# The first two k tiles' modulation taken singly, with a new written order for the opening of a two-layer block kernel

## The chip, the cores and the metric

The kernel runs on one core of one Trainium2 chip. The metric is device time of one execution in microseconds (us), the median of several runs; a profiled execution of the same kernel gives the trace. The core has TensorE (PE; its weight loads are shown apart as PEld), VectorE (DVE), ScalarE (ACT), GpSimd (POOL) and SyncE (SP), which here issues most of the transfers.

## The reference, cut to what matters

The reference is two layers of a diffusion block over 256 latent tokens and 256 context tokens of width 1024: in each layer a gated feed-forward stage, a mixer (a short convolution in layer 0, grouped attention in layer 1) and a second feed-forward stage. Before each stage the tokens are normed and modulated by vectors that come from a conditioning vector. The change touches the opening: the first modulation, norm and feed-forward product of layer 0.

```
def _rms(t, g):
    t32 = t.astype(jnp.float32)
    y = t32 * lax.rsqrt(jnp.mean(t32 * t32, axis=-1, keepdims=True) + NORM_EPS)
    return y.astype(t.dtype) * g
def _modulate(t, g, shift, scale):
    return _rms(t, g) * (1 + scale) + shift
def _swiglu(h, w13, w2):
    gte, up = jnp.split(h @ w13, 2, axis=-1)
    return (jax.nn.silu(gte) * up) @ w2
...
        mod = (jax.nn.silu(c) @ mod_w[i] + mod_b[i]).reshape(bsz, 3, 3, 1, D_MODEL)
        modc = (jax.nn.silu(c_ctx) @ mod_w[i] + mod_b[i]).reshape(3, 3, D_MODEL)
        lat = lat + 0.5 * mod[:, 0, 2] * _swiglu(_modulate(lat, norm_g[i, 0], mod[:, 0, 0], mod[:, 0, 1]), ffn_w13[i, 0], ffn_w2[i, 0])
```

The same weights serve latent tokens (with `c`) and context tokens (with `c_ctx`), so every modulation product has two rows.

## The kernel before

Tokens lie transposed: `x` is [128, 8, 512], that is eight k tiles of 128 features with 256 latent and 256 context tokens side by side. Every fp32 product is made of three products of rounded halves: an operand is split into a high part (`wh`, `hh`; ACT) and the rest (`wl`, `hl`; DVE), and high x high, high x low and low x high are added up in PSUM.

The first feed-forward stage begins with three w13 blocks, i = 0, 1, 2, each with two PSUM tiles, `pg` and `pu`. Their products go over eight k tiles, taken as q = 0..3 (pairs) and j = 0, 1, with k = 2q + j.

Elsewhere a scheduler sets the order of instructions; in this opening a hand-written order does, the string `FIRST_STEPS` (L39), for TensorE, VectorE, ScalarE and the SP queue. Each engine runs its instructions in that order, and a waiting one holds up all behind it. A step is a letter with digits:

- `L` chq: `mod_load` (L913), two transfers of 512 KB with the columns of modulation chunk ch (0 is shift, 1 is scale) for the two k tiles of pair q, from `in_mod0`.
- `P` chq: `mod_pe` (L918), the product of these 256 columns with the conditioning vector. The eight k slices of the contraction go to four 32-column strips of the array (`tile_position`), in two rounds; fp32 takes two passes each, so one P is 16 passes of 256 columns. ACT then copies the result to `row`.
- `T` chq: `mod_turn` (L934), two small products per pair with `rowsum` that add the four strips and turn the row into columns; DVE adds the bias and writes `A00` (1 + scale) or `B00` (shift, named `mod` in the trace).
- `R` i half: `first_raw` (L1020), a 512 KB transfer of half a w13 block. `W` i p: `first_w` (L1031), the split of 512 of its columns, one ACT and one DVE instruction.
- `X`: `first_inv` (L950), the inverse rms spread over the partitions by PE, and ACT's copies of it, `ris`, for the two token halves.
- `U` q: `scale_q` (L958), x times norm gain times `ris` on DVE, four instructions for a pair, into `hr`.
- `N` qj: `norm_one` (L968), the modulated tile of one k: ACT writes `hh`, DVE (or ACT, for j = 1 and q > 0) the full value, DVE the rest `hl`.
- `h`, `w`, `l` with iqj: `first_part` (L994), two products each for one k tile: high x high, low weights, low tokens. `M` iq: all twelve of block i and pair q.
- `F` and the `WARM` matmuls before the list: `fill` (L894), products of a tile of ones into an unused PSUM tile, two passes each. `S` loads the conditioning vectors for later.

Before the list come the fill and `rms_sum` (L270), which sums squares with PE and takes root and reciprocal. PSUM has a pool of six tiles (`psum`) and one of two (`psmall`). The two sums lie in the small pool until ACT has copied `ris`; P10's result goes to the large pool, P00's to the small one.

## Time and profile before

| | |
|---|---|
| median of 3 runs | 1567.11 us (1566.95 to 1568.15) |
| profiled execution | 1566.27 us |
| its span in the profile | 1564.5 us |
| TensorE clock granted | 1.00 |
| read from memory | 259.45 MB, 167 GB/s over the span |

In the trace each group of instructions has its line, engine, output and inputs; times are from the start of the span. A matmul's time includes its way through the array, so neighbours overlap, and their spacing is taken from their starts or from the chain of waits, where each piece begins where the one before it ends. A few per cent of the matmul records can be missing.

### The profile page before, as it was taken

Reading aid. Unit: us, or ns where it says so; the run is one execution under the profiler, and the core shown is the slowest. Engines: PE = TensorE matmul, PEld = TensorE weight load, DVE = VectorE, ACT = ScalarE, POOL = GpSimd, SP = SyncE. Lnnn points to the kernel's source line nnn. Section 1 sums busy time; section 2 is a strip of 40 time slices with the busy share of each in tenths; the row PEclk is TensorE's granted clock in tenths of the full one; section 3 lists DMA queues with packets and bytes.
Section 4 is the critical chain, followed back from the end, with each engine's and each line's share of the span. In section 5 each row is a group of like instructions: output and inputs, shape, how many; then the busy total and the mean of one; then the engine's idle time right before and its main releaser. Section 6 shows DMA issues by size and latency. Waiting matters only on the chain.

```text
span 1564.5 us, 26382 instructions
## 1 busy us (share of the span) xinstructions
PE 1552.8 (99%) x10296; PEld 1422.4 (91%) x10296; DVE 1284.7 (82%) x2029; ACT 775.2 (50%) x1297; POOL 224.7 (14%) x188
## 2 busy tenths in 40 slices
PE   9999999999999999999999999999999999999999
PEld 7898998999888899989999899989999899898888
DVE  5789789889987588978978888978978788888676
ACT  5642453545323465436435475436445456674553
POOL 0012304100000111132131111131131002300000
PEclk9999999999999999999999999999999999999999
DMA  9567567564665525665665635665765743277562
GB/s 370 195 187 203 133 174 195 136 186 141 190 191 177 124 67 149 189 161 125 196 160 139 188 84 135 194 164 120 257 164 155 236 151 118 85 238 218 171 197 74
DMA packets 88254, 263.53 MB, mean 168 GB/s; under 512 B 10817, under 2 KB 12609, under 8 KB 88129
## 3 DMA queue, kind: packets, MB, share of 16 engines
q1 hardware_dynamic: 69408, 230.72, 46.1%
q0 software_dynamic: 16128, 29.37, 11.4%
q10 hardware_dynamic: 2592, 1.76, 0.4%
q8 instruction: 80, 1.31, 0.3%
q14 instruction: 46, 0.37, 0.1%
HBM read 259.45 MB, written 1.05 MB: 167 GB/s over the span
## 4 chain that ended last, share of the span: by engine, by line
PE 83%; DVE 9%; DMA 3%; ACT 2%; issue 2%; POOL 0%; POOLq 0%; DVEq 0%; ACTq 0%; SPq 0%
PE py L138 7%; PE py L137 7%; PE py L139 7%; PE p L137 6%; PE p L138 5%; PE p L139 5%; PE q L137 4%; PE q L139 4%; PE q L138 4%; DVE junk L178 2%; PE py L145 2%; PE pu L145 2%; PE pg L145 2%; DMA wr<-in_modT 2%; DVE wl L109 2%
## 5 line engine op out<-in xcount | busy, mean ns | idle before, releaser
L108 ACT ACTIVATE wh<-wr 128x1024 fp32r<-128x1024 f32 (+2 forms) x446 | 394.6, 913 | 329.6 <-PE py L138 123.3
L109 DVE TENSOR_TENSOR wl<-wr,wh 128x1024 fp32r<-128x1024 f32 (+2 forms) x446 | 459.0, 1053 | 91.6 <-ACT wh L108 73.0
L178 DVE CUSTOM_DVE_ANT_0 junk<-wr,scbc,modb 128x1024 bf16<-128x1024 f32 x213 | 275.0, 1291 | 49.3 <-DMA wr<-in_modT 46.8
L138 PE MATMUL py<-gl,wh 128*128 128x512 f32 (+1 forms) x570 | 213.4, 374 | 0.1
L137 PE MATMUL py<-gh,wh 128*128 128x512 f32 (+1 forms) x570 | 213.5, 375 | 0.0
L139 PE MATMUL py<-gh,wl 128*128 128x512 f32 (+1 forms) x570 | 213.0, 374 | 0.0
L704 POOL TENSOR_SCALAR wr<-wr 128x512 f32<-128x512 f32 x56 | 100.1, 1788 | 708.3 <-DMA wr<-in_w 474.4
L567 DVE SCALAR_TENSOR_TENSOR x<-py,mod,x 128x256 f32<-128x256 f32 x213 | 94.2, 478 | 51.8 <-PE py L139 40.8
L137 PE MATMUL p<-th,wh 128*128 128x256 f32 x448 | 126.8, 283 | 0.0
L138 PE MATMUL p<-tl,wh 128*128 128x256 f32 x448 | 126.8, 283 | 0.0
L139 PE MATMUL p<-th,wl 128*128 128x256 f32 x448 | 126.8, 283 | 0.0
L139 PEld LDWEIGHTS py<-gh,wl 128*128 128x128 f32 x570 | 107.3, 188 | 19.2
L138 PEld LDWEIGHTS py<-gl,wh 128*128 128x128 f32 x570 | 107.4, 188 | 18.5 <-DVE gl L109 0.5
L137 PEld LDWEIGHTS py<-gh,wh 128*128 128x128 f32 x570 | 107.4, 188 | 18.4
L115 POOL DMA_DIRECT2D w4l<-in_w x56 | 52.2, 932 | 283.2 <-ACT w4l L114 205.7
L137 PE MATMUL q<-bh,wh 128*128 128x256 f32 x320 | 90.9, 284 | 1.6 <-ACT wh L108 0.8
L139 PE MATMUL q<-bh,wl 128*128 128x256 f32 x320 | 90.9, 284 | 0.4 <-DVE wl L109 0.3
L138 PE MATMUL q<-bl,wh 128*128 128x256 f32 x320 | 90.5, 283 | 0.0
L138 PEld LDWEIGHTS p<-tl,wh 128*128 128x128 f32 x448 | 86.0, 192 | 0.3
L137 PEld LDWEIGHTS p<-th,wh 128*128 128x128 f32 x448 | 86.0, 192 | 0.3
L139 PEld LDWEIGHTS p<-th,wl 128*128 128x128 f32 x448 | 86.0, 192 | 0.0
L764 ACT ACTIVATE sg<-sg 128x512 f32<-128x512 f32 x56 | 35.4, 631 | 88.8 <-DVE sg L763 88.7
(304 smaller groups left out, 4081.2 us busy)
## 6 DMA issues: line engine op xcount, KB each, us to landing
wr<-in_w SPq DMA_DIRECT2D x120, 512.0 KB, 4.7
wr<-in_modT SPq DMA_DIRECT2D x117, 512.0 KB, 4.9
wr<-in_w2b SPq DMA_DIRECT2D x64, 448.0 KB, 4.1
wr<-in_w2a SPq DMA_DIRECT2D x32, 512.0 KB, 4.8
wr<-in_w SPq DMA_DIRECT2D x56, 256.0 KB, 3.5
wr<-in_w POOLq DMA_DIRECT2D x56, 256.0 KB, 4.7
w4l<-in_w POOLq DMA_DIRECT2D x56, 256.0 KB, 6.1
pm<-in_mod SPq DMA_DIRECT2D x16, 512.0 KB, 10.4
```

What stands on the lines that cost most here:

```text
L108: nc.scalar.activation(out=hi, in_=src, func=AF.Copy)
L109: return nc.vector.tensor_tensor(out=lo, in0=src, in1=hi.bitcast(F32), op=ALU.subtract)
L115: nc.gpsimd.dma_start(out=lo, in_=src, accum_op=ALU.add)
L137: nc.tensor.matmul(ps, wh, mh, start=first, stop=False, **kw)
L138: nc.tensor.matmul(ps, wh, ml, start=False, stop=False, **kw)
L139: nc.tensor.matmul(ps, wl, mh, start=False, stop=last, **kw)
L145: nc.tensor.matmul(ps, w[0], m[2], start=first and n == 0, stop=False)
L178: nc.vector.tensor_tensor_reduce(out=junk, in0=raw, in1=scbc[:, v, :], scale=0.5 if ch in (2, 8) else 1.0, scalar=modb[:, l, col : col + 1 ...
L567: ins = nc.vector.scalar_tensor_tensor(out=x[:, m, s * S : s * S + S], in0=ps[:, o : o + S], scalar=g[:, m, s : s + 1], in1=x[:, m, s * S ...
L704: nc.gpsimd.tensor_scalar(out=r1[:, :T2], in0=r2[:, :T2], scalar1=-1.0, scalar2=None, op0=ALU.mult)
L764: nc.scalar.activation(out=self.sg, in_=self.sg, func=AF.Silu)
```

## The change

The modulation of k tiles 0 and 1 is now loaded, multiplied and turned one k tile at a time: a transfer of 512 KB from a new layout, `in_mod1`, brings the 128 columns of one k tile of one chunk with all eight k slices (step J), one product makes 16 passes of 128 columns (Q), and one product with `rowsum` turns it (V). The pairs from q = 1 on are as before. `scale_q` can take one k tile alone. The written order is new up to the first steps of q = 1. Two fill matmuls fewer are run first.

```
-WARM = 39
+WARM = 37
...
-    "L10 L00 R00 R10 P10 X U0 L11 P00 L01 T10 T00 W00 N00 W01 N01 F h000 w000 l000 R20 W10 "
-    "W11 h001 w001 h100 h101 l001 l100 l101 U1 P11 L12 P01 L02 T11 T01 w100 w101 N10 N11 W20 "
+    "J10 J00 R00 J11 J01 R10 Q10 Q00 W00 X U00 L11 V10 V00 W01 N00 F h000 Q11 Q01 L01 U01 w000 "
+    "l000 V11 V01 W10 W11 h100 w100 N01 l100 h001 w001 l001 R20 h101 w101 l101 U1 P11 L12 P01 "
+    "L02 T11 T01 N10 N11 W20 "
     "W21 U2 M01 R01 R11 P12 L13 P02 L03 T12 T02 M11 R21 N20 N21 W02 W03 M20 W12 W13 U3 M21 "
     "P13 P03 T13 T03 W22 W23 M02 N30 N31 M12 M22 M03 M13 M23 S"
...
-        pr = psum("pr") if (ch, q) == (1, 0) else psmall("pr")
+        pr = psmall("pr")
...
+    def one_load(ch, k):
+
+        rows["one", ch, k] = raw = hot("pm", F32)
+        nc.sync.dma_start(raw, a["mod1"][ch, k])
+
+    def one_pe(ch, k):
+        raw = rows["one", ch, k]
+        pr = psmall("pr") if k else psum("pr")
+        for i in range(KT):
+            g = 32 * (i % 4)
+            nc.tensor.matmul(
+                pr[g : g + 32, :P], sccol[:, i, :], raw[:, i * P : i * P + P],
+                start=(i < 4), stop=(i >= 4), tile_position=(0, g),
+            )
+        row = tp.tile([P, T2], F32, name=nm("row"), tag="gm", bufs=3)
+        nc.scalar.copy(row[:, :P], pr[:, :P])
+        rows["one", ch, k] = pr, row
+
+    def one_turn(ch, k):
+        pr, row = rows["one", ch, k]
+        nc.tensor.matmul(pr[:, S : S + 2], row[:, :P], rowsum, start=True, stop=True)
+        nc.vector.tensor_tensor(
+            out=(A00 if ch else B00)[:, k, :], in0=pr[:, S : S + 2],
+            in1=(sb1[:, k : k + 1] if ch else modb[:, 0, k : k + 1]).to_broadcast([P, 2]),
+            op=ALU.add,
+        )
...
-    def scale_q(q):
-        for s in range(2):
-            h32[q, s] = gp.tile([P, T2], F32, name=nm("hr"), tag="gl" if s else "gh")
-        for k in range(2 * q, 2 * q + 2):
+    def scale_q(q, j=None):
+
+        if j != 1:
+            for s in range(2):
+                h32[q, s] = gp.tile([P, T2], F32, name=nm("hr"), tag="gl" if s else "gh")
+        for k in range(2 * q, 2 * q + 2) if j is None else (2 * q + j,):
...
+    m1 = mw[0][:, : 2 * D].reshape(KT, P, 2, KT, P)[:, :, :, :2]
+    d["mod1"] = m1.transpose(2, 3, 1, 0, 4).reshape(2, 2, P, D)
```

The list of steps gains the letters J, Q and V for the three new functions. The products themselves, their number and their operands are the same; before, the first order placed `w100` and `w101` behind T11 and T01, and the new one places them ahead of P11.

More of the change, by code (lines that the diff above doesn't have):

```diff
@@ L1037, in hybrid_kernel @@
     steps = {
+        "J": one_load,
+        "Q": one_pe,
+        "V": one_turn,
         "P": mod_pe,
```

## The prediction

> **What bounds the kernel now.** I read the page first: which engine is full.

> ```profile
> PE 1552.8 (99%) x10296; PEld 1422.4 (91%) x10296; DVE 1284.7 (82%) x2029; ACT 775.2 (50%) x1297; POOL 224.7 (14%) x188
> ```

> TensorE sets the end. Then the windows, because the change touches only the first 30 us or so.

> ```profile
> 10.00:20.00 10.00, 9.76 (x94) 7.86 (x93) 4.77 (x15) 6.66 (x14) 0.00 (x0) 1.00 1.01 385
> 20.00:30.00 10.00, 9.09 (x65) 6.06 (x64) 6.17 (x17) 4.03 (x10) 0.00 (x0) 1.00 1.02 414
> 30.00:44.00 14.00, 14.00 (x87) 10.61 (x88) 11.34 (x27) 8.79 (x18) 0.00 (x0) 1.00 1.03 408
> 44.00:60.00 16.00, 16.00 (x98) 12.52 (x97) 12.41 (x25) 11.76 (x19) 0.00 (x0) 1.00 0.67 227
> 100.00:155.00 55.00, 55.00 (x309) 48.34 (x308) 54.72 (x82) 19.59 (x27) 11.59 (x8) 1.00 0.70 203
> ```

> Columns: window, its length, busy time of PE, PEld, DVE, ACT, POOL with their counts, granted clock, DMA share, GB/s. From 30 us on PE has no idle time; before that it waits. So what counts is when the block M01 (12 products of the first w13 block with k tiles 2 and 3) starts: later work follows back to back, and a shift of M01 is a shift of the end. Third, the chain of waits from 16 to 31 us (start, time, engine and line), which shows what puts M01 at 29.93.

> ```profile
> 16.98 1.16 PE pr L938 x8
> 18.42 1.10 ACT hh L973 x2
> 19.55 0.41 DVE hr L979
> 19.97 0.67 DVE hl L987 x2
> 20.63 0.61 DVE wl L109
> 21.29 0.50 PE pu L1000
> 25.23 0.23 PE pu L1000
> 25.46 1.86 PE pr L926 x32
> 27.32 0.54 PE pr L938 x4
> 27.87 0.62 PE pr L938 x4
> 28.59 0.17 DVE mod L943
> 28.78 1.10 ACT hh L973 x2
> 29.93 0.50 PE pg L1000
> ```

> A product costs 0.23 us. P11 with P01 (32 passes) costs 1.86, T11 with T01 1.16, and then M01 waits for mod and hh. Last, the timeline of what leads to the first product.

> ```profile
> 10.78 0.76 DVE L266 TENSOR_TENSOR acc<-acc,sq 128x256 f32<-128x256 f32 x2 [0.61 <-ACT sq L258]
> 13.73 1.07 PE L926 MATMUL pr<-pm,sccol 128*32 128x256 f32 x16
> 14.13 0.17 DVE L284 RECIPROCAL ri<-rs 128x2 f32<-128x2 f32 x1 [0.73 <-ACT rs L280]
> 14.73 1.16 PE L293 MATMUL ss<-ident,ri 128*128 128x128 f32 x8
> 15.48 0.82 ACT L953 COPY ris<-ss 128x256 f32<-128x256 f32 x2 [0.19 <-PE ss L293]
> 15.89 1.72 DVE L963 SCALAR_TENSOR_TENSOR hr<-x,normg,ris 128x256 f32<-128x256 f32 x4 [1.59 <-ACT ris L953]
> 17.70 0.63 ACT L108 ACTIVATE wh<-wr 128x512 fp32r<-128x512 f32 x1 [0.24 <-DMA wr<-in_w]
> 18.36 0.69 DVE L109 TENSOR_TENSOR wl<-wr,wh 128x512 fp32r<-128x512 f32 x1
> 19.57 0.50 PE L1000 MATMUL pg<-hh,wh 128*128 128x512 f32 x1 [0.23 <-ACT hh L973]
> ```

> After the sums come P10, X (L293), the ris copies, P00, T10 with T00, hh, and the first product at 19.57.

> **The change, part by part.** *Two fill matmuls less.*

> ```profile
> 1.50:5.00 3.50, 3.50 (x18) 3.50 (x18) 1.00 0.89 279
> 6.00:9.50 3.50, 3.50 (x33) 3.50 (x33) 1.00 1.02 340
> 11.96 0.28 PE L275 MATMUL ss<-ones,acc 128*128 128x1 f32 x2
> ```

> These windows count fill passes alone: 0.106 us each once the start is over, four passes less are 0.42 us. The sums move from 11.96 to 11.54, which is when acc is done (10.78 + 0.76), so all of it is gained: Q10 starts at 13.3 where P10 started at 13.73, and ri is ready at 13.9, not 14.3.

> *Q10 and Q00 for P10, ahead of X.* That is 32 passes of 128 columns for 16 of 256. The trace has no such pass. Upper bound: the price of P11 with P01, 1.86 us for 32 passes of 256. Lower bound: four passes on four column strips run side by side, as one fill pass of 128 columns does at 0.106, so 8 x 0.106 plus the 0.3 us that a P block has beyond its passes, 1.2 us. I take 1.2, because the columns are halved and a fill pass has both the width and the weight columns of four strips. X then starts at 14.5 (14.73 before); ri no longer holds it.

> [...]

> *W00 ahead of X.* R00 goes from ninth to seventh of the 512 KB transfers. Before, ACT waits for it until 17.70; at 385 GB/s a place is worth 1.36 us, so it lands near 15.0. ACT, in order, does two row copies (to about 14.95), then wh of W00 (0.63, to 15.6), then ris: 15.6 to 16.4, 0.1 later than before, since W00 now stands in front. DVE takes wl of W00 (0.69, to 16.3), two hr (1.72 / 4 each, to 17.15) and the two additions (0.17 each, to 17.5); V10 and V00 on PE are done by 16.2. So hh starts at 17.55 where it started at 18.42: **0.87 us gained**, the first product at 18.70. This is the gain, since P00 and T00 no longer follow ris, and hr has two tiles in place of four.

> *Q11, Q01, V11, V01 behind the first two products.*

> ```profile
> 20.93 1.14 ACT L108 ACTIVATE wh<-wr 128x512 fp32r<-128x512 f32 x2
> 22.47 1.29 DVE L109 TENSOR_TENSOR wl<-wr,wh 128x512 fp32r<-128x512 f32 x2
> 25.07 0.39 PE L1000 MATMUL pu<-hl,wh 128*128 128x512 f32 x1
> 25.39 1.93 PE L926 MATMUL pr<-pm,sccol 128*32 128x256 f32 x32
> 28.34 0.48 PE L1000 MATMUL pg<-hh,wl 128*128 128x512 f32 x1
> ```

> The step from a product to a P block is 0.32 (25.07 to 25.39), 0.09 over a product, so the Q block costs 0.09 + 1.2; after two products from 18.70 it brings w000 to 20.45. Its wl (18.2) and hl (19.75) are ready. Four products, the first 0.50 after the break, bring V11 to 21.65. Four passes of V are half of 1.16, **0.58**, and mod is added at 22.33 to 22.5. DVE is in order: the wl pair of W10 and W11 stands behind that addition, 1.29 us, to 23.8. That is a new wait. Behind it w100 waits on PE, idle from about 22.7 but for one product. (ACT's wh pair, behind the row copies, is done by 22.1 and is not it.) From 23.8 fifteen products are left, 0.50 + 14 x 0.23 = 3.7: the P11 block follows at 27.5, where the chain has 25.46.

> *The four products w100 and w101 move ahead of P11.* Before, they stand at 28.34, in the 1.5 us in which PE waits for mod and hh (28.49 to 29.93), and so cost nothing. Ahead of P11 they cost 4 x 0.23 = **0.92**, and the wait they covered stays: P11 to M01 is still 4.5 us.

> *The sum*: gain 0.87; Q block 1.29, V block 0.58, four products 0.92; idle PE between first product and P11 1.29 before (25.46 - 19.57 - 20 x 0.23) and 1.41 after (27.5 - 18.70 - 24 x 0.23 - 1.29 - 0.58). -0.87 + 1.29 + 0.58 + 0.92 + 0.12 = **+2.0 us**, M01 near 31.95. The profiled execution took 1566.27 us (span 1564.5), so 1568.3 in its place; the median shown is 0.84 above it, so 1569.1.

> *Costed at nothing.* The transfers from L11 on keep their places (ten 512 KB transfers ahead of them as before), so DMA brings the rest no later, and SP and POOL get as many instructions as before. pr of (0, 0) moves to the larger PSUM pool, and one pu takes the fill's buffer, whose last writer, the fill, is over by then. The scheduler leaves the later order alone but for two small moves on DVE near 46 us, where the addition of T13 now stands ahead of one subtotal of the w13 blocks:

> ```profile
> 46.13 0.69 DVE L465 TENSOR_TENSOR hr<-hr,hr 128x512 f32<-128x512 f32 x1
> ```

> Mod and hh of the last two k tiles come up to 0.69 us later by it, behind the 36 products of M02, M12 and M22 (8.3 us); without that cover it would cost the 0.69.

> *Bounds.* If no idle time were left between first product and P11, the sum is 2.0 - 1.41 = +0.6. If both Q blocks cost 1.86, X comes 0.7 later and so does w000 again: +3.4.

> **The rivals.** *The lead is kept (faster).* PE idles 1.29 us between 19.57 and P11 and 0.67 more ahead of M01; if Q and V (1.87) fell wholly into these, only the 0.87 would remain: 1566.2. It decides if M01 starts before 29.1. For it: the added work is no larger than the idle time. Against: the wait for mod and hh ahead of M01 loses its four products, so it can't shrink.

> *Halved columns, full price.* The Q blocks cost 1.86 each: +3.4, 1570.5. For it: each strip's load is as wide as before. Against: the fill row.

> *Something later swallows the delay*, the change does nothing that shows: 1567.1. For it: DVE is busy 54.72 of 55 us from 100 to 155 and might pace PE there. Against: PE has 55.00 busy in the same row, and DVE itself starts those blocks later.

> *The clock.* The fill ran 18 passes in 3.5 us at the start and 33 later. If the gap of 1.5 us that now stands ahead of M01 brought the slow pace back for one such stretch, it would cost another 3.5 x (1 - 18/33) = 1.6: 1570.7. Against: the wait of 0.67 ahead of M01 did not do so before, where the clock column says 1.00. [...]

> **How the numbers follow.** Forecast 0.60, full price 0.20, swallowed 0.09, lead kept 0.06, clock 0.05. A measurement can tell about 0.2% from no change, 3.1 us: slower begins at 1570.2, faster ends at 1564.0. Slower: the clock case, two thirds of the full price, and a tenth of the forecast (waits mis-sized by over 1 us): 0.25. No case reaches 1564.0; 0.02 is kept for what I have not seen. The runs shown reach from 0.2 below to 1.0 above their median. The forecast's own range is 1567.5 (its lower bound, less 0.2) to 1570.1 (1.0 above it); the range reaches on to 1566.6, between the two cases below, and to 1571.4, the full price with 0.9 of the runs' spread.

> **What would show it.** First product near 18.7; a Q block of 1.2 us, not 1.9; w100 waiting for wl near 23.8; P11 near 27.5 and M01 near 31.95, with over 1 us of idle PE ahead of it; from there every stage the same length. I am wrong if M01 starts before 29.9, or if a later stage changes its length by over 0.5 us.

## The result, and the profile after

The changed kernel took 1571.61 us (median of 8 runs, 1570.57 to 1574.32) against 1566.95 us (8 runs, 1565.09 to 1568.37): ratio 1.0035 [1.0026, 1.0044]. Forecast were 1569.1 us and a range to 1571.4. The profiled execution took 1572.09 us, its span is 1570.3.

First the opening, which the prediction worked out. From the timeline of the changed kernel (start, time, engine, line, operation; L277 are the sums, L946 Q, L295 X):

```profile
12.36 0.28 PE L277 MATMUL ss<-ones,acc 128*128 128x1 f32 x2
14.14 1.08 PE L946 MATMUL pr<-pm,sccol 128*32 128x128 f32 x32
15.15 1.16 PE L295 MATMUL ss<-ident,ri 128*128 128x128 f32 x8
16.02 0.69 ACT L982 COPY ris<-ss 128x256 f32<-128x256 f32 x2
23.03 0.50 PE L1031 MATMUL pg<-hh,wl 128*128 128x512 f32 x1 [0.29 <-DVE wl L111]
```

From its chain of waits (start, time, engine and line; L1031 are the products, L956 V, L928 P11 with P01, L967 T11 with T01):

```profile
17.81 1.10 ACT hh L1004 x2
...
18.96 0.50 PE pg L1031
19.45 0.23 PE pu L1031
19.69 1.01 PE pr L946 x32
20.70 0.43 PE pg L1031
...
21.82 0.35 PE pr L956 x4
...
22.28 1.30 DVE wl L111 x2
...
27.32 1.86 PE pr L928 x32
29.18 0.54 PE pr L967 x4
29.73 0.62 PE pr L967 x4
...
30.45 0.17 DVE mod L972
...
30.64 1.10 ACT hh L1004 x2
...
31.79 0.50 PE pg L1031
```

The first product comes at 18.96, M01 at 31.79, where they came at 19.57 and 29.93: 0.61 earlier and 1.86 later. Q is 1.01 on the chain, not 1.86; the wl pair stands at 22.28 behind the second mod; 1.45 us of idle PE stand ahead of M01. So far the trace follows the forecast (18.70, 1.2, 22.33 to 23.8, 31.95).

The first row of its page, and its windows (window, length, busy time of PE, PEld, DVE, ACT, POOL with counts, granted clock, DMA share, GB/s); then before for the last three windows:

```profile
PE 1552.9 (99%) x10324; PEld 1423.6 (91%) x10324; DVE 1287.0 (82%) x2031; ACT 776.9 (49%) x1299; POOL 226.3 (14%) x188
```

```profile
30.00:44.00 14.00, 12.55 (x83) 9.38 (x83) 10.14 (x25) 10.00 (x20) 0.00 (x0) 1.00 1.03 408
44.00:60.00 16.00, 16.00 (x99) 12.49 (x98) 12.94 (x27) 10.05 (x15) 0.00 (x0) 1.00 0.56 190
100.00:155.00 55.00, 55.00 (x317) 48.66 (x316) 54.75 (x82) 19.37 (x27) 11.23 (x8) 1.00 0.71 211
553.00:563.00 10.00, 9.10 (x75) 8.75 (x74) 6.87 (x16) 3.66 (x10) 2.43 (x2) 1.00 0.41 101
840.00:850.00 10.00, 9.26 (x75) 8.85 (x74) 8.63 (x13) 5.42 (x11) 0.86 (x1) 1.00 0.62 157
985.00:1000.00 15.00, 13.43 (x112) 13.23 (x111) 11.81 (x16) 8.13 (x15) 0.87 (x1) 1.00 0.58 144
```

```profile
553.00:563.00 10.00, 9.70 (x82) 9.56 (x81) 7.33 (x20) 6.75 (x16) 2.43 (x2) 1.00 0.28 55
840.00:850.00 10.00, 9.97 (x83) 9.77 (x82) 7.94 (x11) 6.49 (x13) 0.86 (x1) 1.00 0.58 160
985.00:1000.00 15.00, 14.69 (x108) 13.84 (x107) 13.90 (x19) 8.16 (x13) 0.87 (x1) 1.00 0.64 193
```

PE has 28 passes more: the four Q take 64 passes of half the width where two P took 32, and four fill passes are gone. So the sums that are formed are the same, as the section on the change says, but the number of passes is not. In the windows from 44 to 155 us PE is full in both kernels. Later it isn't: in the last two windows it idles 0.74 and 1.57 us where it idled 0.03 and 0.31, though these stages are the same (a window is fixed in time, so it holds work some us apart in the two kernels). Laying the starts of the same matmuls side by side takes that away: the changed kernel is 1.89 us behind at 160 us, 1.45 at 225, 2.65 at 360, 3.36 at 850 and 5.72 at 1000, and 5.8 at the end: steps of some tenths to 1.3 us at a few places, some of them gains. From the waits of PE between 45 and 1550 us (operation, what it waited for, us in total, times, longest), after and before:

```profile
PE q L139 <- ACT gm L759: 2.9, 5, 1.6
```

```profile
PE q L137 <- ACT gm L757: 1.1, 3, 0.4
```

In the forecast's terms: M01 comes as late as it said, and in this execution 3.9 us more are lost behind it, where it said nothing would change.

### The profile page after: what moved, and what is told of

The parts are those of the page before. It is cut to its first block, busy times and chain, and to the rows that moved or that the text cites. A ratio compares the mean times of both kernels' runs of the same rounds, so it can differ in the third digit from the quotient of the medians.

```text
span 1570.3 us, 26445 instructions
## 1 busy us (share of the span) xinstructions
PE 1552.9 (99%) x10324; PEld 1423.6 (91%) x10324; DVE 1287.0 (82%) x2031; ACT 776.9 (49%) x1299; POOL 226.3 (14%) x188
## 4 chain that ended last, share of the span: by engine, by line
PE 89%; DVE 6%; ACT 3%; DMA 1%; issue 1%; POOL 0%; POOLq 0%; ACTq 0%; DVEq 0%; SPq 0%
PE py L139 9%; PE py L140 9%; PE py L141 9%; PE p L139 6%; PE p L140 6%; PE p L141 6%; PE q L139 5%; PE q L141 5%; PE q L140 4%; PE py L147 2%; PE pu L147 2%; PE pg L147 2%; PE py L149 1%; DVE wl L111 1%; PE pg L149 1%
## 5 line engine op out<-in xcount | busy, mean ns | idle before, releaser
L139 PEld LDWEIGHTS py<-gh,wh 128*128 128x128 f32 x570 | 107.4, 188 | 18.2
```

Of the source, the lines that this page charges most:

```text
L139: nc.tensor.matmul(ps, wh, mh, start=first, stop=False, **kw)
```

## The experiments

Every run compared a kernel with before on the same chip. The table gives, for each profiled execution, the passes on PE, when x's fourth transfer ends, when the first product and M01 start, the time from M01 to the end of the span, then the ratio of times with its interval, and how often in an execution the clock fell for one stretch of 3.41 us: the granted clock is recorded with every timed run, and one stretch at half clock in 1565 us takes 0.0011 from its mean. Landing times in the expectations are counted from 0.25 us before the profile's zero; here they are counted from the zero. "M01 to the end" in them is likewise 0.25 shorter than in the table.

| kernel | passes | x ends | first product | M01 | M01 to end | ratio to before | stretches |
|---|---|---|---|---|---|---|---|
| before | 10296 | 10.01 | 19.57 | 29.93 | 1534.6 | | 0.2 |
| changed | 10324 | 10.57 | 18.96 | 31.79 | 1538.5 | 1.0035 [1.0026, 1.0044] | 1.5 |
| e1 changed again | 10324 | 11.50 | 20.40 | 34.08 | 1534.4 | 1.0021 [1.0008, 1.0034] | 1.6 |
| e2 before, delayed | 10306 | 10.21 | 20.39 | 33.12 | 1532.2 | 1.0015 [1.0003, 1.0027] | 0.4 |
| e3 changed, 28 passes fewer | 10296 | 10.97 | 19.86 | 32.72 | 1533.9 | 1.0016 [1.0004, 1.0027] | 1.1 |
| e4 cover back | 10324 | 10.56 | 19.50 | 31.63 | 1536.3 | 1.0028 [1.0016, 1.0039] | 1.7 |
| e5 before, input not bound | 10296 | 9.44 | 19.08 | 29.42 | 1535.7 | 1.0005 [0.9996, 1.0014] | 0.1 |
| e6 changed, strided | 10324 | 11.32 | 20.41 | 33.27 | 1534.8 | 1.0034 [1.0021, 1.0047] | 1.3 |
| e7 before again | 10296 | 9.76 | 19.24 | 29.59 | 1536.1 | 0.9999 [0.9989, 1.0009] | 0.0 |
| e8 before, less fill | 10292 | 9.64 | 19.37 | 29.75 | 1532.0 | 0.9996 [0.9988, 1.0005] | 0.1 |
| e9 before, input bound | 10296 | 10.81 | 19.97 | 30.31 | 1532.9 | 0.9996 [0.9987, 1.0005] | 0.2 |
| e10 changed, in in_mod0 | 10324 | 8.88 | 18.25 | 31.08 | 1536.3 | 1.0025 [1.0015, 1.0035] | 1.7 |
| e11 before, reads in_mod1 | 10296 | 10.06 | 20.33 | 30.68 | 1531.5 | 0.9999 [0.9990, 1.0007] | 0.3 |
| e12 before, 28 passes more | 10324 | 10.93 | 20.55 | 30.89 | 1534.2 | 1.0020 [1.0009, 1.0030] | 0.9 |
| e13 the same elsewhere | 10324 | 10.46 | 19.42 | 29.78 | 1534.8 | 1.0023 [1.0012, 1.0034] | 0.7 |
| e14 as e3 | 10296 | 11.66 | 19.90 | 32.72 | 1536.3 | 1.0027 [1.0016, 1.0037] | 1.8 |
| e15 changed, array busy | 10324 | 10.25 | 20.63 | 33.48 | 1536.1 | 1.0034 [1.0021, 1.0048] | 0.6 |
| e16 both | 10296 | 10.75 | 20.17 | 33.04 | 1533.9 | 1.0026 [1.0015, 1.0036] | 0.6 |
| e17 before, 28 fewer | 10268 | 10.76 | 21.20 | 31.52 | 1531.9 | 0.9992 [0.9984, 1.0001] | 0.2 |
| e18 before, 48 fewer | 10248 | 10.39 | 19.56 | 29.91 | 1535.4 | 1.0016 [1.0006, 1.0026] | 0.8 |

**First four: the passes, a delay, the moved products.** After the first result three theories stood: A, that the added TensorE instructions shift where in the program its instruction fetches fall (80 transfers of 16 KB in before's trace, in the median 0.97 us long and 256 of PE's matmuls and weight loads apart); B, that the later loss is chance; C, that a later M01 itself costs more later.

e1 is the changed kernel itself.

> The changed kernel once more, for a second trace of it. What it settles: the first trace had M01 1.86 us later than before, as forecast (2.0), but its span 5.8 us longer; 3.9 us were lost in many steps of 0.2 to 1.0 us after 280 us. Theory A (the added PE instructions move the points at which code is fetched, and with that which transfers are late): the stalls after 280 us stand at the same places, and the median is 4 to 6 us above before. Theory B (the later losses are chance of one execution): the places change, and the median over the rounds is 1.5 to 3 us above before. Theory C (a later start of M01 costs more later on, because waits grow): like A, same places.

e2 puts idle matmuls behind w101 of before:

```
-... T11 T01 w100 w101 N10 ...
+... T11 T01 w100 w101 D N10 ...
+        "D": lambda: (big(3), fill(2)),   # big: matmul(idle, ones, x[:, 0, :]), 512 columns
```

> The kernel before with 3 fill matmuls of 512 columns and 2 of 128 put on PE ahead of M01, and nothing else: about 2.5 us of PE work into an idle time of 0.67, so M01 starts 1.8 to 2.1 us later, with only 10 PE passes more. Theory A (place of the code): +1.9 us over before, 1.4 to 2.6. Theory C (a late M01 costs more later): +4 to +6. Theory B: +1.9.

e3 shortens the changed kernel's fill in instructions, not in time:

```
-        fill(WARM)
+        fill(WARM - 19)
+        big(5)
```

> The changed kernel with 19 of the fill matmuls at the start replaced by 5 of 512 columns, which is 28 PE passes fewer, so that each later PE instruction stands at the place in the code where it stood before the change. Theory A: the later losses go, +1.5 to +2.5 us over before. Theory C and B: as the changed kernel in the same rounds, +4 to +6 by C.

e4 puts the four products back behind the turns:

```
-... W10 W11 h100 w100 N01 ... R20 h101 w101 l101 ... T11 T01 N10 ...
+... W10 W11 h100 N01 ... R20 h101 l101 ... T11 T01 w100 w101 N10 ...
```

> The changed kernel with w100 and w101 put back behind T11 and T01, where they stood before; all else as changed. The four products again lie in the wait for mod and hh: M01 starts 0.9 us earlier than in the changed kernel (near 30.9), if my sum is right. On the whole time: 0.9 us less than the changed kernel by the sum alone; by theory A the later stalls stay, by theory C they shrink with the delay (2 us less).

e1 is slower again, but by less, and its M01 is 2.3 us later than the first trace's. From M01 to the end it took no longer than before did (1534.4 and 1534.6), where the first trace took 1538.5: most of the 3.9 us lost there was that one execution's. Its median is 3.3 us above before, between A's 4 to 6 and B's 1.5 to 3, and of A's "same places" only some come back (845 us, below; not the 1.6 us near 1000). In e2's trace M01 is 3.2 later, of which 0.8 is there at the first product, ahead of the edit; the 2.4 that are left are about what it costs in time (1.0015, or 2.4 us). So a delay is paid about once, and C falls. e3 lies below e1 by less than their intervals. In e4 M01 came only 0.16 earlier than in the changed kernel, though x landed at the same time. Its timeline:

```profile
19.50 0.50 PE L1031 MATMUL pg<-hh,wh 128*128 128x512 f32 x1 [0.49 <-ACT hh L1004]
...
24.11 0.50 PE L1031 MATMUL pg<-hh,wh 128*128 128x512 f32 x1 [0.35 <-ACT hh L1004]
...
25.51 0.50 PE L1031 MATMUL pg<-hl,wh 128*128 128x512 f32 x1 [0.19 <-DVE hl L1018]
...
27.09 1.93 PE L928 MATMUL pr<-pm,sccol 128*32 128x256 f32 x32
...
31.63 0.50 PE L1031 MATMUL pg<-hh,wh 128*128 128x512 f32 x1 [0.42 <-ACT hh L1004]
```

Here the first product itself came 0.54 later (19.50 for 18.96), in an execution whose clock was at half from 14.13 to 17.54 us. Counted from the first product, P11 starts after 7.59 us where it took 8.29 in the changed kernel, and M01 after 12.13 where it took 12.83: 0.70 earlier. That is no chance of one execution, since seven traces of the new order agree on the way from the first product to M01 within 12.82 to 12.87 (the eighth, e1, took 13.68, with its clock at half until 22.3 us). So the four products cost 0.7 of their 0.92 ahead of P11; the other 0.2 goes into new waits for hh and hl that their absence leaves there.

**x's landing.** In the six traces then at hand x's fourth transfer ended later in the four kernels with the new order. The rows of ACT's squares in before, e1 and e10 show the spread (the wait ahead of them in brackets):

```profile
10.12 1.15 ACT L258 ACTIVATE sq<-x 128x512 f32<-128x512 f32 x2 [1.24 <-DMA x<-in_xT]
```

```profile
11.60 1.15 ACT L260 ACTIVATE sq<-x 128x512 f32<-128x512 f32 x2 [2.40 <-DMA x<-in_xT]
```

```profile
8.99 1.16 ACT L260 ACTIVATE sq<-x 128x512 f32<-128x512 f32 x2 [0.18 <-DMA x<-in_xT]
```

e5 lists in_mod1 among before's inputs (two lines in the layout); e6 lays it out with rows 8 KB apart; e7 is before unchanged; e8 is before with `WARM = 37`.

> The kernel before, with the new input in_mod1 among its inputs but no instruction that reads it. In the five traces so far the last of x's four transfers landed at 10.26 and 10.46 us in the two kernels without the change and at 10.81 to 11.75 in the four with it, and everything up to M01 follows from it. Theory P (the new input moves the other inputs in memory, and the fourth transfer of x lands later by it): landing at 10.8 or later, M01 (29.93 in the first trace of before) at 30.5 or later, time 0.5 to 1.5 us above before. Theory J (the contiguous reads of in_mod1 right behind x slow it): landing near 10.3 as before, time as before. Theory B (single packets of x stall at random in every execution): landing anywhere from 10.2 to 11.8, time within 0.5 us of before.

> The changed kernel, with in_mod1 laid out so that its transfers read rows of 4 KB that lie 8 KB apart, as those of in_mod0 do, instead of one contiguous piece. Theory J: x's fourth transfer lands near 10.3, the first product comes near 18.4 and M01 near 31.2, time 0.5 to 1.5 us below the changed kernel's. Theory P: landing at 10.8 or later, time as the changed kernel. Theory B: landing anywhere from 10.2 to 11.8, time as the changed kernel, ratio to before about 1.002 to 1.0035.

> The kernel before, unchanged, as a measure of what the comparison itself gives. All theories: a ratio of 1.000 within 0.1%. Theory B besides: its trace differs from the first trace of before by steps of about 1 us at the same places of the feed-forward stages (near 175, 334, 553, 843, 905, 992 us) where the changed kernel's did, with both signs, and by 1 us or more at the end of the span. If the later stages match the first trace to within 0.5 us throughout, theory B falls and the changed kernel's later losses are its own.

> The kernel before, with the change's one small edit alone: two fill steps less. By my prediction's first step the sums start 0.42 us earlier and follow acc directly, P10 starts when its transfer and the sums allow, and the first product and M01 come at most 0.4 us earlier; the time moves by less than 0.5 us. If the fill set more than that, the time moves by more. If x lands late in this trace (10.8 or later), the sums wait for it and nothing is gained, which speaks for theory B, since neither the inputs nor their transfers differ from before.

The reads' stride brings nothing: e6 lands at 11.32 and takes 1.0034. e5 did not test its theory, since an input that nothing reads was left out of the program (its trace has a fetch of 208 bytes at the start, as before's has, where the changed kernel's has 216). e7 returns 0.9999, and yet its trace differs from the first one by steps of up to 1.2 us, both ways, so chance in the later stages is real, though it averages out. So the next three: e9 binds the input by a late transfer of 1 KB (`nc.sync.dma_start(spare, a["mod1"][0, 0, :, :2])`), e10 keeps the new order and reads its data from a longer in_mod0, e11 lets before's L10 and L00 read in_mod1, so that the first two k tiles get the modulation of other columns.

> The kernel before with in_mod1 as an input that it really has: one transfer of 1 KB from it is issued behind the first feed-forward's prologue, and nothing uses it. (In e5 nothing read the input, so the program did not have it: the start-up fetch of its list of addresses was 208 bytes as in before, and 216 in the changed kernel.) In the ten traces so far x's fourth transfer ends at 9.69 to 10.46 us in the five kernels without the change and at 10.81 to 11.75 in the five with it. Theory P (the 27th input moves the inputs in memory): 10.8 or later, first product at 20.2 or later, M01 at 30.5 or later, time 1 to 2 us above before. Theory J (it is the reads of the two half-width transfers behind x): 9.7 to 10.5, time as before. Theory B (chance): anywhere.

> The changed kernel with the data of in_mod1 appended to in_mod0 as a fifth group, so that the program has the 26 inputs of before and J10 to J01 read from in_mod0; the computation is the same. Theory P: x's fourth transfer ends at 9.7 to 10.5, the first product comes at 18.7 to 19.2, M01 at 31.5 to 32.2, and the time is about 2 us above before (ratio 1.001 to 1.002), which is the sum of my prediction. Theory J: x ends at 10.8 or later, M01 at 32.0 to 34.3, ratio 1.002 to 1.0035. Theory B: x ends anywhere, ratio as for the changed kernel.

> The kernel before with its first four modulation transfers (L10 and L00) read from in_mod1, so that their data are the weights of other columns, and the modulation of the first two k tiles is not the reference's; sizes, order and all instructions are those of before. Theories P and J: x's fourth transfer ends at 10.8 or later, the first product at 20.2 or later, M01 at 30.5 or later, time 1 to 2 us above before. If x ends at 9.7 to 10.5 here and late in e10, neither the inputs nor what stands behind x does it, and the rest of the change (its instructions, or where R00 stands) is the cause. Theory B: anywhere.

e9 lands late and e11 does not; both cost nothing in time. e10 has x at 8.88, the earliest of all, its first product at 18.25 and M01 at 31.08, and still 1.0025. So x's landing is not what the time lacked, and neither input nor source address is the cause of it. It varies by 2.8 us between executions; whether the new order shifts it is open (six traces of it, the changed kernel, e1, e3, e6, e10 and e14, average 10.82; nine of before's order, without e2 and e17, 10.17).

**The passes alone.** e12 adds 28 passes to before in the fill, e13 ahead of the first product:

```
+    def strips(n):
+        for i in range(n):
+            g = 32 * (i % 4)
+            nc.tensor.matmul(idle[g : g + 32, :P], ones[:, :32], ones, start=True, stop=True, tile_position=(0, g))
...
-        fill(WARM)
+        fill(WARM - 4)
+        strips(18)
```

(e13: `WARM = 38` and `"F": lambda: strips(20)`.) e14 is e3 once more.

> The kernel before with 28 passes more on TensorE, as many as the change adds, at next to no time: four fill steps (8 passes, 0.85 us) give way to 36 passes on column strips (nine groups of four at 0.109 us as in the Q block, 0.98 us). Over the thirteen traces so far, the stretch from M01 to the end took 1533.4 us on average (standard deviation 1.7) in the eight kernels that have 10292 to 10301 passes, the changed kernel with 28 passes fewer and a plain delay of before among them, and 1535.8 (1.6) in the five with 10324, at the same work. Theory A (the later loss hangs on where in the program TensorE's fetches of its own instructions fall): M01 within 0.5 us of before, but M01 to the end 1535 to 1537; no stall at 610 to 640 us, where four of eight had one of 1.2 to 1.8, and stalls near 570, 855, 915 or 1000 us in their place; time 1.5 to 2.5 us above before, ratio 1.001 to 1.0016. Theory B (chance): ratio 0.9995 to 1.0005, M01 to the end 1531 to 1536. Theory C (the later M01 itself costs more later): as before, ratio 0.9995 to 1.0005.

> The same 28 passes more, put elsewhere: 40 strip passes in place of the five fill steps ahead of the first product (10 passes), and one fill step less at the start. Theory A: as in e12, ratio 1.001 to 1.0016, M01 to the end 1535 to 1537, since from the first product on the program is shifted by the same 28 passes. Theories B and C: ratio 0.9995 to 1.0005.

> The changed kernel with 28 passes fewer in its fill, once more (e3: ratio 1.0016, 1.0004 to 1.0027; the changed kernel and its variants with all 10324 passes: 1.0035, 1.0021, 1.0028, 1.0034, 1.0025). Theory A: ratio 1.001 to 1.002, the sum of my prediction without the later loss, and M01 to the end near 1533.5. Theories B and C: ratio 1.0025 to 1.0033 and M01 to the end near 1535.8.

28 passes that compute nothing used, in the order of before, cost 0.20% and 0.23% in two places; e13's M01 is 0.15 earlier than before's. Of the stalls that A expected, two are in e12's trace, 10 to 15 us ahead of where it had them: 0.85 us of idle PE between 845 and 848, 0.83 near 555, where before has 0.03 and 0.30; there is none at 610 to 640, and near 915 and 1000 there is hardly more than in before (0.79 and nothing, for 0.64 and 0.32). M01 to the end missed A's 1535 (1535.3 in the table's count): it took 1534.2 and 1534.8, within what before itself took (1531.5 to 1536.1 with e5, e7, e8, e9 and e11), so these two traces don't show the loss that the times show; both profiled executions lay below their medians. The part from 840 to 850 us, one row each from the windows of e12, e18 and e17:

```profile
840.00:850.00 10.00, 9.15 (x75) 8.75 (x74) 8.63 (x14) 5.51 (x10) 0.86 (x1) 1.00 0.63 165
```

```profile
840.00:850.00 10.00, 8.63 (x68) 8.02 (x67) 8.63 (x14) 5.50 (x10) 0.86 (x1) 1.00 0.62 164
```

```profile
840.00:850.00 10.00, 10.00 (x86) 10.00 (x85) 8.03 (x11) 6.49 (x12) 0.86 (x1) 1.00 0.47 122
```

e12 nearly repeats the row of the changed kernel, with the order of before; e18 (below) idles more, e17 not at all. Over all twenty traces PE idles 0.74 to 1.37 us between 840 and 853 in the changed kernel, e1, e4, e12 and e15, which have 10324 passes, and in e18 with 10248. It idles 0.03 or nothing there in the eleven with 10268 to 10306 passes, and in e6, e10 and e13, also with 10324. e13 has other stalls of about 1 us near 315 and 905 us.

e14 missed A's number: 1.0027 where 1.001 to 1.002 was expected. Its own trace has a possible reason, a third cause. The windows and the start of M01 in e14:

```profile
29.82:33.23 3.41, 1.95 (x18) 1.51 (x11) 1.26 (x5) 2.02 (x5) 0.00 (x0) 1.00 1.03 411
33.23:36.64 3.41, 3.41 (x9) 2.61 (x9) 2.86 (x7) 2.45 (x5) 0.00 (x0) 0.50 1.02 399
36.64:40.05 3.41, 3.41 (x43) 2.03 (x42) 1.59 (x5) 0.74 (x2) 0.00 (x0) 1.00 1.03 411
```

```profile
32.72 0.50 PE L1036 MATMUL pg<-hh,wh 128*128 128x512 f32 x1 [1.45 <-ACT hh L1009]
...
33.76 0.63 PE L1036 MATMUL pu<-hh,wl 128*128 128x512 f32 x1
34.18 0.63 PE L1036 MATMUL pg<-hl,wh 128*128 128x512 f32 x1
...
37.25 1.07 PE L933 MATMUL pr<-pm,sccol 128*32 128x256 f32 x16
```

Half a microsecond behind the start of M01 the granted clock falls to 0.50 for 3.41 us, and products follow each other in 0.43 us instead of 0.23. M01 to P12 takes 4.53 us where it takes 3.17 in the first trace of the changed kernel (31.79 to 34.96): 1.36 us lost. e10 and e6 have such a stretch 0.3 and 1.6 us behind M01, and the traces e1, e3, e4, e6, e10 and e14 of the new order have one that begins between 14 and 16 us (in e1 of twice the length); the first trace has none. No trace of before's order up to e13 has any before the end of the span; e17 later had one, at 14 us. e6 and e16 have one more at 560 us and e10 at 909, each right behind stalls of PE of 0.5 to 1.5 us in all, so the two may not be independent; no run varies a stall by itself.

**The clock, and the number of passes.** e15 gives the array work in its two thin stretches, e16 also takes 28 passes away:

```
-        fill(WARM)
+        fill(30)
+        big(3)
...
-    "J10 J00 R00 J11 J01 R10 Q10 ... L02 T11 T01 N10 ..."
+    "J10 J00 R00 J11 J01 R10 H Q10 ... L02 T11 T01 G N10 ..."
+        "G": lambda: (big(1), fill(2)),
+        "H": lambda: big(1),
```

(e16: `fill(12)`, `big(7)`.) e17 and e18 are before with `fill(20)`, `big(5)` and with `fill(13)`, `big(6)` and `big(1)` at F.

> The changed kernel with its TensorE passes kept at 10324, but with work for the array in its two thin stretches: one 512-column matmul between the sums and Q10, one with two fill steps between T01 and M01 (where PE waits 1.45 us for mod and hh), and a fill of 8.9 us in place of 7.8 at the start. In the traces the granted clock falls to 0.5 for 3.41 us at a time, and each such stretch follows a window of 3.41 us in which few columns went through the array (16 to 1424 effective columns in ten of thirteen, where no window of before has under 1680). From the clock recorded with every run the changed kernel and its variants have 1.6 such stretches in an execution, before 0.2; a fit over 245 runs gives 0.9 us for each, 1.5 for the new order and 1.6 for the 28 passes. Theory K (the clock is a part of the loss): 0.3 such stretches in an execution or fewer, M01 at 32 to 33.5, time 1.0 to 1.5 us below the changed kernel, ratio 1.0015 to 1.0025. If the stretches go and the time stays (1.0025 to 1.0035), the clock is a companion and not a cause; if the stretches stay, their tie to the work of the array falls.

> As e15, and with 28 passes fewer, so that TensorE's passes number 10296 as before. Theories K and A together (clock and place of the instruction fetches account for what my sum lacked): 0.3 low stretches or fewer, ratio 1.0007 to 1.0016, that is the 1 to 2 us of the new order alone. If it stays above 1.002, a third cause is left.

> The kernel before with 28 passes fewer: 38 of 78 fill passes give way to ten of 512 columns, about as long. Theory A (the place of the fetches matters, not the number of passes): a ratio other than 1 by up to 0.002, of either sign, and stalls at other places than in before. If instead more passes simply cost more (0.06 us each by e12 and e13): ratio 0.9985 to 0.9992. If e12 and e13 were slower for their strips and not for their number: 0.9995 to 1.0005.

> The kernel before with 48 passes fewer (fill steps replaced by 512-column matmuls at the start and ahead of the first product). As e17: by theory A any ratio within 0.002 of 1; by the number of passes 0.9975 to 0.999, and then the fastest kernel here; by neither 0.9995 to 1.0005.

The stretches fell from 1.6 to 0.6 in both, so the clock followed the work of the array here. The time did not fall (1.0034, 1.0026), and both missed their expectations; by its own, e16 leaves a third cause. M01 came at 33.48 and 33.04, later than the mean of the new order (32.61). From the first product on they are as fast as the others (12.85 and 12.87), so it is the first product that is late, behind the matmuls added ahead of Q10 and X. e15's expectation would read a time that stays as the clock being a companion of the loss and not a cause; with M01 later than meant, its time can't decide that. These two runs show that more work for the array held the clock up, not what that is worth. (The "ten of thirteen" stretches in e15's expectation are nine of twelve; the other three followed windows of 2056 to 3076 columns.)

e17 with 28 passes fewer is not slower, e18 with 48 fewer costs 0.16%. So it is neither the number of passes nor the strips. It isn't a shift in time by itself either: in e11 and e17 the first product comes 0.8 and 1.6 us later than in before, at no cost. Nor is it the clock alone, though e12, e13 and e18 have 0.9, 0.7 and 0.8 stretches against 0.2: a stretch of 3.41 us at half clock can lose no more than half of that, 1.7 us, which makes 1.2 of e12's 3.1, and the executions without any stretch are slower too (medians 1567.7 in three of e12 and 1569.4 in four of e13, 1564.3 in 22 of before beside them). What is left is where the later instructions stand in the program; that is argued by leaving out the rest, and no run varies it by itself. No kernel here is shown to beat before.

## Why the prediction was wrong

Point by point. *Fill*: the gain of 0.42 is not to be seen; alone it moves the time by less than can be told (e8, 0.9996), and in the changed kernel x landed 0.56 later, so that the sums start at 12.36, not 11.54. *Halved columns*: 32 passes of 128 columns took 1.08 where 32 of 256 take 1.93; the price halves, and the rival of the full price falls. Both have 32 weight loads of the same width, and 2 x 1.08 - 1.93 = 0.23 us is all that does not halve with the columns. In the changed kernel's trace the first 32 loads, 0.11 us each, lie from 14.13 to 14.94, beside the passes from 14.14 to 15.22. *X, ris, hh, first product*: 15.15, 16.02, 17.81 and 18.96 for 14.5, 15.6, 17.55 and 18.70, each later by 0.26 to 0.65, as x landed later. *Q and V blocks*: 1.01 and 0.35 on the chain for 1.29 and 0.58. *The wl pair* as the new wait: right, to 23.58 for 23.8. *P11 and M01*: 27.32 and 31.79 for 27.5 and 31.95. *The four moved products*: 0.92 was forecast, and e4 shows 0.7.

Over several executions the size holds too: M01 averages 32.61 in six traces of the new order (the changed kernel, e1, e3, e6, e10, e14) and 30.03 in nine of the old one (before, e5, e7, e8, e9, e11, e12, e13, e18), 2.58 apart, of which 0.65 is the difference in x's landing in the same executions; if that passes on whole, which is not shown, 1.9 is left of the 2.0 forecast. That this comes so close is in part luck, since two terms are off in opposite ways: the first product gains nothing on average (19.63 for 19.68, where 0.87 was forecast), and from it to M01 the new order takes 2.5 us more (12.8 for 10.3 to 10.4), where 2.9 was forecast.

The step that failed is the last one, "from there every stage the same length", with the clock rival's chance of 0.05 that rests on it. From M01 to the end six traces of the new order with 10324 passes (the changed kernel, e1, e4, e6, e10, e15) average 1536.0 us, seven of before's with 10292 to 10306 (before, e2, e5, e7, e8, e9, e11) 1533.6: about 2.5 us were lost where nothing was forecast. Two things go with this loss.

*The granted clock.* The rival had the size: behind a gap of 1.45 us ahead of M01 the slow pace came back for one stretch in e14, 1.6 us by the forecast, 1.36 measured, though not in every execution: the first trace has the same gap and no such stretch. Its argument against (before, a wait of 0.67 did no harm) looked at the gap and not at the whole stretch from P11 to M01: 4.5 us in which column strips, 2-column products and the gap put few columns through the array (2064, a strip's pass counted as a quarter, for 4112 before). Before, four products of 512 columns and a shorter gap stood there. Where the stretches begin differs from execution to execution, so it hits some and not others: 1.6 stretches in each against 0.2. Within the runs of one and the same kernel, each stretch goes with 0.82 us (standard error 0.14, 329 runs), about 1.4 x 0.82 = 1.1 us for the change; that this is all cause and not in part company is not shown. Nor was PE idle all through the time ahead of it: in e14 it was busy 1.95 of the 3.41 us before 33.23.

*The place of the instructions.* The forecast counted the 28 added passes by the time of Q and V and nothing more. e12 and e13 show that such passes cost 3.1 to 3.6 us in the order of before, and e17 and e18 that it isn't their number. That it is the place of what follows, and that before was at a good place, is argued from that and from the stall near 845 us, not shown. That the fetches of instructions are the link fits (28 passes with their loads are 56 of the 256 between two fetches), but no run shows it.

The parts don't add up neatly, and the cause of the later loss stays open in part: e3 and e14 (order without passes) average 1.0022, e12 and e13 (passes without order) 1.0022, the changed kernel, e1, e6 and e10 together 1.0029. So how much of the changed kernel's own loss is the clock and how much the passes is open.

## What to carry to other kernels

Don't take an added matmul to cost its own time alone: in a kernel whose PE is 99% busy a padding of 28 useless passes moved the time by 0.2%, so a change of this size has to be compared with padded copies of before. When independent wide products are moved out of a stretch of narrow ones, look at what is left for the array over the whole stretch, not at the longest gap alone: work put into the two thin stretches here took the times at half clock from 1.6 to 0.6 in an execution (e15, e16). Count a step from the event that it hangs on, here the first product: e4's gain of 0.7 looks like 0.16 on the clock of its own execution. And compare several profiled executions before reading steps of 1 us in a long trace: two of the same kernel differ by as much.
